# Four of five pairs kept raw at the border of two FFN stages, and the last pair's stores begun two steps later

## The chip, the cores and the metric

The kernel runs on one core of one Trainium2 chip. The metric is device time in microseconds: the median of three runs before the change is 2650.71 us (2648.62 to 2653.48). One execution was also recorded by the hardware profiler; durations, waits and transfers below are from it.

Engines: PE is TensorE (matmul; PEld its weight load), DVE is VectorE, ACT is ScalarE, POOL is GpSimd, and SP only issues transfers. Each engine works its instructions off in order, and so do the two queues of transfers, one issued by SP and one by POOL.

## The reference

One inference step of a one-layer encoder for 640 tokens (512 of a prompt and 8 x 16 samples), width 2048, in fp32:

```python
def merge_and_ffn(x, oa, ob, norm_grp_a, norm_grp_b, w_out, norm_ffn, w_gate, w_up, w_down):
    o = jnp.concatenate([rmsnorm(oa, norm_grp_a), rmsnorm(ob, norm_grp_b)], axis=-1)
    x = x + o @ w_out
    h = rmsnorm(x, norm_ffn)
    return x + (jax.nn.silu(h @ w_gate) * (h @ w_up)) @ w_down
```

Before this stands an input projection with two groups of attention heads, behind it a final norm. The change is in the last line: h @ w_gate and h @ w_up (FF1 here, 2048 to 5632) and the product with w_down (FF2, 5632 to 2048).

## The kernel before

**Split operands.** Every fp32 operand x is cut into two halves that are kept as float32r: hi = x rounded by an ACT copy, lo = x - hi by a subtraction on DVE. A product then takes three matmuls, hi x hi, hi x lo and lo x hi (`mm3`, lines 204, 205 and 206). Weights are split by `split` (line 195 on ACT, line 196 on DVE). Line 200 is the same subtraction with a gain, used elsewhere.

**Seven products for eight.** FF1 and FF2 multiply 2 x 2 blocks by a Strassen-Winograd scheme: `quartet` loads four weight blocks b11, b12, b21, b22 (line 907), forms their differences (lines 920 and 922 on DVE, 925 and 934 on POOL) and runs seven products p1, p6, p7, p2, p5, p4, p3. Each product splits its weight combination, runs k x 3 matmuls of 128x128 by 128x320 against operand number `which` (0 to 6), and yields. The caller then adds the product's bank into its results on DVE (line 944), copying the first one on ACT (line 1003 in FF1, 1084 in FF2).

**FF1.** The 44 row blocks of w_gate and w_up make 22 pairs i of two blocks. For each pair there is one quartet for w_gate and one for w_up, with k = 8: 168 matmuls each. After w_up, the gated result (lines 1030 to 1036) is turned into the seven Winograd combinations that FF2 needs as operands (lines 1040 to 1043 and in place); they are the seven `parts` of the pair, each 128x320 fp32, kept in S tiles.

**Storing parts.** `store_part` stores one part. It is called once when the parts have been formed, and from then on after the products of what follows (in FF1 all but p1, in FF2 all). For an ordinary pair it copies hi into a scratch tile of the tag "half" (line 985, ACT; the tag has two buffers), subtracts lo in place (line 987, DVE) and issues two transfers of 160 KB from SP into `act_d` (lines 988 and 989). For a pair in `raw_pairs` it issues one transfer of 160 KB into `first_d` (line 981) and splits nothing. The S tiles of a part go back to their list as soon as its store is emitted.

**FF2.** 32 steps. Step t works on 8 output rows q = t % 8 in turn, with the pairs in `active(t)`: five or six pairs, each staying for eight consecutive steps modulo 32. `active(0)` is [0, 1, 2, 3, 4]; pair 21, the last that FF1 forms, is first wanted in step 23, pair 0 again in step 25. With five pairs a product has k = 5, 15 matmuls, and a step 105. Operands stay in S tiles (hi and lo side by side) while their pair is active. When a pair comes in, `fetch` loads hi and lo together, 320 KB, by a transfer from POOL (line 951). In steps 0 to 7, x2 is loaded too (lines 1073 and 1074).

**The border.** While the last FF1 quartet runs, each of its seven products frees eight S tiles of h; `free(which)` (the hook `after` of that quartet) fills them with the operands `which` for step 0. Raw pairs are loaded from `first_d`, two to a transfer from SP (line 961, 320 KB; 160 KB where one is left over), and split by ACT (line 966) and, line 967, by DVE for the first of the two and POOL for the second. The others are fetched ready (line 951). Since a raw pair's halves were never stored, a raw pair that leaves in steps 0 to 7 is written to `act_d` then (line 1066, 320 KB from SP), as pairs 0 to 4 are wanted again in steps 25 to 31.

**What sets the order.** The source emits instructions, and the framework's planner orders them for each engine: an instruction with its operands ready may go ahead of one emitted before it on the same engine. It inserts the waits as well. Transfers from SP use eight completion counters in turn, so a transfer is issued only when the one eight before it has landed. Two rules bear on this place. `keep_turns` keeps the users of an S or W tile in their order. `keep_behind` ties each ACT copy of line 985 behind the ACT instruction emitted last before it, so that it can't go ahead of it.

Of the kernel before, what the change touches and what calls it, by code (L numbers as in the profile page):

```python
# [13 lines left out]
P = 128  # L14
# [3 lines left out]
HT = 320  # L18
# [15 lines left out]
def active(step):  # L34

    return [j for j in range(NPAIR) if (step - START[j]) % STEPS < 8]
# [13 lines left out]
class Net:  # L50
# [20 lines left out]
    def add(self, queue, work):  # L71
        self.queues.setdefault(queue, []).append(work)
# [209 lines left out]
def sh(t, *shape):  # L282
    v = t[:, :int(np.prod(shape))]
    if len(shape) == 2:
        v = v.rearrange("p (a b) -> p a b", a=shape[0])
    elif len(shape) == 3:
        v = v.rearrange("p (a b c) -> p a b c", a=shape[0], b=shape[1])
    return v
# [7 lines left out]
def r(ap):  # L296
    return ap.bitcast(F32R)


def build(nc, tc, io, pools):  # L300
# [14 lines left out]
    def dram(name, shape):  # L315
        return pools["dr"].tile(list(shape), F32, tag=name, name=name)
# [486 lines left out]
    own_b, acts_b = group_operands(ob_d, g_b, ssq, range(8))  # L803
    n.add("decode", decode_a(1))
    x2_d, act_d = dram("x2_d", (KT, P, TOK)), dram("act_d", (7, P, NPAIR, 2, HT))
    first_d = dram("first_d", (7, P, 3, HT))
    r_a, ssq_a = n.get("S"), n.get("S")
    for m in range(KT):
        ps = n.dense([(io["w_out_b"][m], 8)], acts_b)
# [141 lines left out]
        nc.gpsimd.dma_start(out=r(sh(t, 2, HT)), in_=r(act_d[which, :, j]))  # L951
        lefts[j][which] = t, hl

    raw_pairs = active(0)[1:4]

    def free(which):
        n.put("S", *(h[which][0] for h in hs))
# [18 lines left out]
    def store_part():  # L976

        if parts:
            j, which, src, done = parts.pop(0)
            if j in raw_pairs:  # L980
                dma(out=first_d[which, :, j - raw_pairs[0]], in_=src)
            else:
                at = n.emitted()
                hi = n.scratch()
                nc.scalar.activation(r(hi), src, AF.Identity)  # L985
                n.behind.append((at, n.emitted()))
                nc.vector.tensor_tensor(r(src), src, hi, ALU.subtract)  # L987
                dma(out=act_d[which, :, j, 0], in_=hi)
                dma(out=act_d[which, :, j, 1], in_=src)
            n.put("S", *done)  # L990

    gate = None
    for i in range(NPAIR):
        for src in ("w_gate", "w_up"):
# [5 lines left out]
            for step, bank in quartet(8, load, hs, (lambda w: next(prep)) if start else None, free if end else None,  # L1000
                                      eng=nc.vector if start else nc.gpsimd):
                if step == "p1":
                    nc.scalar.activation(c11, bank, AF.Identity)
                elif step == "p6":
                    y.append(n.get("S"))
                    c12, c22 = y[1][:, :HT], y[1][:, HT:]
                    add(c12, c11, bank)
                elif step == "p7":
                    add(c21, c12, bank)
                elif step == "p5":  # L1010
                    add(c22, c21, bank)
                    add(c12, c12, bank)
                elif step == "p2":
                    add(c11, c11, bank)
                elif step == "p4":
                    add(c21, c21, bank)
                elif step == "p3":
                    add(c12, c12, bank)
                if step != "p1":
                    store_part()  # L1020
# [31 lines left out]
    def fetch_waiting(left):  # L1052
        while len(waiting) > left:
            for j, which in waiting.pop(0):
                fetch(j, which)

    def step(t, part="all"):
        now = active(t)
        nxt = active(t + 1) if t + 1 < STEPS else []
        cnt, q, last = len(now), t % 8, t >= STEPS - 8  # L1060

        def after(which):
            gone = [j for j in now if j not in nxt]
            for j in gone:
                if j in raw_pairs and t < 8:
                    dma(out=act_d[which, :, j], in_=sh(lefts[j][which][0], 2, HT))
            n.put("S", *(lefts[j][which][0] for j in gone))
            waiting.append([(j, which) for j in nxt if j not in now])
            fetch_waiting(2)

        if t < 8:
            x, y = n.get("S"), n.get("S")
            dma(out=x, in_=x2_d[q])
            dma(out=y, in_=x2_d[q + 8])
            sums.append((x, y, n.get("S") if q % 2 == 0 else sums[-1][2]))
        x, y, u = sums[q]
        c11, c21, c12, c22 = x[:, :HT], x[:, HT:], y[:, :HT], y[:, HT:]
        us = u[:, HT * (q % 2):HT * (q % 2) + HT]
        o = 2 * sum(len(active(i)) for i in range(q, t, 8))
        load = lambda z: io["w_down"][q + 8 * (z % 2), :, o + cnt * (z // 2):o + cnt * (z // 2) + cnt]  # L1080
        for name, bank in quartet(cnt, load, [lefts[j] for j in now], None, after, part):
            if name == "p1":
                if t < 8:
                    nc.scalar.activation(us, bank, AF.Identity)
                else:
                    add(us, us, bank)
                add(c11, c11, bank)
            elif name == "p6":
                add(us, us, bank)
                if last:  # L1090
                    for c in (c21, c22, c12):
                        add(c, c, us)
            elif name == "p7":
                add(c21, c21, bank)
                add(c22, c22, bank)
            elif name == "p5":
                add(c22, c22, bank)
                add(c12, c12, bank)
            elif name == "p2":
                add(c11, c11, bank)  # L1100
            elif name == "p4":
                add(c21, c21, bank)
            elif name == "p3":
                add(c12, c12, bank)
            store_part()
            yield name

    def run(*args):
        for _ in step(*args):
            pass  # L1110
# [39 lines left out]
    for name in step(STEPS - 2, "late"):  # L1150
        if name == "p2":
            next(norm)
# [107 lines left out]
```

## Time and profile before

| | |
|---|---|
| median of 3 runs | 2650.71 us (2648.62 to 2653.48) |
| profiled execution | 2653.13 us, its span 2651.3 us |
| PE busy | 2586.9 us (98%), 17565 matmuls |
| DVE, ACT, POOL busy | 1982.9, 1069.5, 658.9 us |
| FF1's last quartet, border and step 0 | about 2022 to 2095 us |
| DMA bytes | 388.47 MB, mean 147 GB/s |

The span runs from the first to the last instruction that the profiler recorded. The profile has a page (busy times, 40 slices of the span, the chain of work that ended last, the costliest groups of instructions, transfers) and views of the trace: busy times of each engine in chosen stretches, waits summed by who waited for whom, groups of instructions by line, and instructions in order of time. In their rows "dn" and "at" are PSUM banks, S and W are the tiles of operands and of weights, "half" is the scratch tile, x_d is x2_d.

### The profile page before, as it was taken

The page shows a single profiled execution, that of the slowest core. Times are in us where ns is not written, and L with a number is a line of the kernel's source. Part 1 is how long each engine was busy: PE and PEld are TensorE (multiplying, and loading weights), DVE is VectorE, ACT ScalarE, POOL GpSimd, SP SyncE. Part 2 cuts the span into 40 slices and gives each one's busy share as a digit, 9 for nine tenths or more (in the row PEclk, how much of TensorE's full clock was granted, in tenths as well). Part 3 has the DMA queues.
Part 4 walks back from the last instruction along what each step waited for, and adds up shares of the span by engine and source line. Part 5 has one row for each costly group of instructions (what it writes and reads, how often), then busy time and mean ns, then how long its engine had stood idle before and what let it go on. Part 6 is the DMA issues. An engine that isn't in the chain of part 4 may idle for free.

```text
span 2651.3 us, 45161 instructions
## 1 busy us (share of the span) xinstructions
PE 2586.9 (98%) x17565; PEld 2529.9 (95%) x17565; DVE 1982.9 (75%) x3071; ACT 1069.5 (40%) x1732; POOL 658.9 (25%) x576
## 2 busy tenths in 40 slices
PE   8999999999999999999999999999999799999997
PEld 8999998999899999999999999999999799999996
DVE  5665566655866888778888888888887677777797
ACT  5443344444633544333343443433444333333343
POOL 0000000000211203333333333233234432333353
PEclk9999999999999999999999999999999899999998
DMA  5322232433655433333443433433436975665655
GB/s 172 105 71 80 89 104 85 131 115 132 219 184 187 157 120 122 116 104 124 139 133 123 142 130 125 141 131 124 148 126 215 365 206 151 176 185 163 189 154 179
DMA packets 178390, 388.47 MB, mean 147 GB/s; under 512 B 21696, under 2 KB 70208, under 8 KB 178176
## 3 DMA queue, kind: packets, MB, share of 16 engines
q1 hardware_dynamic: 152832, 329.22, 38.4%
q0 software_dynamic: 24192, 55.06, 7.4%
q8 instruction: 138, 2.26, 0.3%
q10 hardware_dynamic: 1152, 1.31, 0.1%
q14 instruction: 76, 0.62, 0.1%
HBM read 301.90 MB, written 82.87 MB: 145 GB/s over the span
## 4 chain that ended last, share of the span: by engine, by line
PE 70%; DVE 6%; DMA 5%; issue 2%; ACT 1%; POOL 0%; SPq 0%; DVEq 0%; ACTq 0%; POOLq 0%
PE dn L204 14%; PE dn L206 14%; PE dn L205 14%; PE at L204 8%; PE at L205 8%; PE at L206 8%; DVE W L196 2%; DMA W<-w_down 2%; PE at L319 1%; DVE S L944 1%; DMA act_d<-half 1%; ACT W L195 0%; DMA S<-first_d 0%; DMA S<-x_d 0%; PE at L395 0%
## 5 line engine op out<-in xcount | busy, mean ns | idle before, releaser
L204 PE MATMUL dn<-S,W 128*128 128x320 f32 x3694 | 1160.9, 314 | 6.2 <-ACT W L195 4.8
L206 PE MATMUL dn<-S,W 128*128 128x320 f32 x3694 | 1148.1, 311 | 17.7 <-DVE W L196 17.7
L205 PE MATMUL dn<-S,W 128*128 128x320 f32 x3694 | 1146.5, 310 | 1.4 <-DVE S L200 1.0
L195 ACT ACTIVATE W<-W 128x1024 fp32r<-128x1024 f32 (+2 forms) x632 | 608.1, 963 | 977.3 <-PE dn L205 533.6
L196 DVE TENSOR_TENSOR W<-W,W 128x1024 fp32r<-128x1024 f32 (+2 forms) x632 | 740.6, 1172 | 91.9 <-ACT W L195 88.2
L206 PEld LDWEIGHTS dn<-S,W 128*128 128x128 f32 x3694 | 695.7, 188 | 23.1 <-DVE W L196 22.0
L204 PEld LDWEIGHTS dn<-S,W 128*128 128x128 f32 x3694 | 696.3, 189 | 18.2 <-ACT W L195 5.8
L205 PEld LDWEIGHTS dn<-S,W 128*128 128x128 f32 x3694 | 696.1, 188 | 4.2 <-DVE S L200 1.6
L204 PE MATMUL at<-S,W 128*128 128x320 f32 x1594 | 494.6, 310 | 5.6 <-ACT W L195 5.6
L206 PE MATMUL at<-S,W 128*128 128x320 f32 x1594 | 495.3, 311 | 2.3 <-DVE W L196 2.2
L205 PE MATMUL at<-S,W 128*128 128x320 f32 x1594 | 494.1, 310 | 0.0
L925 POOL TENSOR_TENSOR W<-W,W 128x1024 f32<-128x1024 f32 (+2 forms) x75 | 158.9, 2119 | 650.2 <-DVE W L196 381.4
L204 PEld LDWEIGHTS at<-S,W 128*128 128x128 f32 x1594 | 300.1, 188 | 6.1 <-ACT W L195 6.1
L206 PEld LDWEIGHTS at<-S,W 128*128 128x128 f32 x1594 | 300.0, 188 | 4.7 <-DVE W L196 4.5
L205 PEld LDWEIGHTS at<-S,W 128*128 128x128 f32 x1594 | 300.1, 188 | 0.0
L944 DVE TENSOR_TENSOR S<-S,dn 128x320 f32<-128x320 f32 x358 | 163.9, 481 | 71.6 <-PE dn L206 71.6
L934 POOL TENSOR_TENSOR W<-W,W 128x1024 f32<-128x1024 f32 (+2 forms) x75 | 162.4, 2165 | 114.8 <-DVE W L196 108.6
L920 DVE TENSOR_TENSOR W<-W,W 128x1024 f32<-128x1024 f32 (+2 forms) x76 | 127.1, 1672 | 69.3 <-DMA W<-w_down 33.8
L944 DVE TENSOR_TENSOR S<-S,at 128x320 f32<-128x320 f32 x262 | 123.4, 481 | 50.7 <-PE at L206 50.0
L951 POOL DMA_DIRECT2D S<-act_d x168 | 91.7, 547 | 185.2 <-PE dn L206 92.7
L922 DVE TENSOR_TENSOR W<-W,W 128x1024 f32<-128x1024 f32 (+2 forms) x76 | 82.2, 1081 | 64.7 <-DMA W<-w_up 34.6
L987 DVE TENSOR_TENSOR S<-S,half 128x320 fp32r<-128x320 f32 x133 | 115.0, 886 | 14.7 <-ACT half L985 12.9
(152 smaller groups left out, 2129.2 us busy)
## 6 DMA issues: line engine op xcount, KB each, us to landing
S<-act_d POOLq DMA_DIRECT2D x168, 320.0 KB, 3.8
W<-w_gate SPq DMA_DIRECT2D x88, 512.0 KB
W<-w_up SPq DMA_DIRECT2D x88, 512.0 KB
W<-w_in SPq DMA_DIRECT2D x66, 512.0 KB
W<-w_down SPq DMA_DIRECT2D x64, 384.0 KB
W<-w_down SPq DMA_DIRECT2D x68, 320.0 KB
act_d<-half SPq DMA_DIRECT2D x133, 160.0 KB
act_d<-S SPq DMA_DIRECT2D x133, 160.0 KB
```

The source lines that it names most:

```text
L195: self.nc.scalar.activation(hi, src, AF.Identity)
L196: self.nc.vector.tensor_tensor(lo, src, f(hi), ALU.subtract)
L204: mm(out, a[0], b[0], start=first, stop=False)
L205: mm(out, a[0], b[1], start=False, stop=False)
L206: mm(out, a[1], b[0], start=False, stop=last)
L920: nc.vector.tensor_tensor(b12[:, w], b12[:, w], b22[:, w], sub)
L922: nc.vector.tensor_tensor(s6[:, w], b11[:, w], b12[:, w], sub)
L925: eng.tensor_tensor(b11[:, w], b22[:, w], s6[:, w], sub)
L934: eng.tensor_tensor(b21[:, w], b21[:, w], s6[:, w], sub)
L944: add = lambda o, a, b: nc.vector.tensor_tensor(o, a, b, ALU.add)
L951: nc.gpsimd.dma_start(out=r(sh(t, 2, HT)), in_=r(act_d[which, :, j]))
L987: nc.vector.tensor_tensor(r(src), src, hi, ALU.subtract)
```

## The change

```diff
@@ -803,7 +803,7 @@
-    first_d = dram("first_d", (7, P, 3, HT))
+    first_d = dram("first_d", (7, P, 4, HT))
@@ -951,7 +951,7 @@
-    raw_pairs = active(0)[1:4]
+    raw_pairs = active(0)[1:]
@@ -1102,7 +1102,8 @@
             elif name == "p3":
                 add(c12, c12, bank)
-            store_part()
+            if t > 1:
+                store_part()
             yield name
```

Two things change. Pair 4 joins pairs 1, 2 and 3 as a raw pair: in FF1 its seven parts are stored unsplit, one transfer each; at the border it comes as the second of a transfer (pairs 1 and 2, then pairs 3 and 4) and is split by ACT and POOL; and its halves are written to `act_d` when it leaves after step 6. Pair 0 alone is fetched ready for step 0. Second, of the last pair's seven parts the first is stored at the end of FF1, as it was; the other six, stored after products of step 0, are now stored after the products of step 2.

## The prediction

> **What bounds the kernel now.** I read the page first.
>
> ```profile
> span 2651.3 us, 45161 instructions
> PE 2586.9 (98%) x17565; PEld 2529.9 (95%) x17565; DVE 1982.9 (75%) x3071; ACT 1069.5 (40%) x1732; POOL 658.9 (25%) x576
> ...
> PE   8999999999999999999999999999999799999997
> ...
> PEclk9999999999999999999999999999999899999998
> GB/s 172 105 71 80 89 104 85 131 115 132 219 184 187 157 120 122 116 104 124 139 133 123 142 130 125 141 131 124 148 126 215 365 206 151 176 185 163 189 154 179
> ```
>
> TensorE (PE) is busy throughout except at the ends and in slice 32 (2055 to 2121 us), where the granted clock drops too and the DMA engines move 365 GB/s against some 130 before it. That is the border between FF1 and FF2, where the change works. Next the busy times by stretch. I cut them at the last FF1 quartet, the gap after it, step 0 (ended by the copy of step 1's first product at 2095.5) and the steps behind. Columns: stretch, length, then busy time and count of each engine, granted clock, DMA share, GB/s.
>
> ```profile
> 2022.00:2060.60 38.60, 33.45 (x209) 31.65 (x207) 27.04 (x33) 17.65 (x32) 26.44 (x28) 0.96 0.89 303
> 2060.60:2064.10 3.50, 0.06 (x1) 0.09 (x1) 3.43 (x6) 1.26 (x3) 2.83 (x4) 0.94 1.11 385
> 2064.10:2095.50 31.40, 21.47 (x110) 19.88 (x111) 18.49 (x29) 8.19 (x15) 13.51 (x20) 0.79 1.10 371
> 2095.50:2111.80 16.30, 15.68 (x107) 15.42 (x106) 11.90 (x19) 5.57 (x10) 3.69 (x3) 1.00 0.99 332
> 2111.80:2128.70 16.90, 15.85 (x106) 15.13 (x105) 11.76 (x18) 5.52 (x10) 5.77 (x7) 1.00 0.97 328
> 2128.70:2145.60 16.90, 16.90 (x117) 16.90 (x117) 12.36 (x21) 5.89 (x10) 5.50 (x7) 1.00 0.75 214
> ```
>
> In the last row PE never stops: 16.90 / 117 = 0.1444 us for a matmul. At that rate the other stretches lose: quartet 38.60 - 209 x 0.1444 = 8.4 us; gap 3.4; step 0 31.40 - 110 x 0.1444 = 15.5; step 1 0.8; step 2 1.6. Together 29.7 us, and half of it lies in step 0. Who waits for whom from 2060 to 2095.5, and on the DMA queue's side, says why (us in total, times, longest):
>
> ```profile
> ACT half L985 <- DMA act_d<-half: 17.0, 4, 7.4
> DVE S L987 <- ACT half L985: 12.9, 5, 6.7
> ...
> PE at L204 <- ACT W L195: 5.1, 1, 5.1
> ...
> PE dn L206 <- DVE W L196: 4.3, 3, 3.3
> ...
> PE dn L204 <- ACT W L195: 3.5, 1, 3.5
> ...
> ACT half L985 <- DVE S L1036: 2.4, 1, 2.4
> ...
> PE at L206 <- DVE W L196: 0.5, 1, 0.5
> ```
>
> ```profile
> SPq L988 <- ACT half L985: 15.5, 5, 5.2
> ```
>
> The parts of the last pair are stored here. L985 copies one into a scratch tile; there are two scratch tiles, so it waits until an earlier store out of that tile has landed. ACT, DVE and the SP queue work in order, and behind L985 stand the weight splits (L195, L196) that PE waits for, behind L988 the loads of w_down. The chain in order of time shows the turns:
>
> ```profile
> 2062.84 0.48 ACT half L985
> ...
> 2063.75 9.20 DMA S<-x_d
> ...
> 2073.02 10.74 DMA act_d<-half
> ...
> 2083.85 0.48 ACT half L985
> ...
> 2084.34 5.45 DMA act_d<-half
> ...
> 2090.79 0.82 DVE W L922
> ```
>
> So a transfer takes 5 to 11 us while the DMA engines are full, and each holds up three queues.
>
> **The parts in step 0, removed.** Six of the seven parts leave it: 6 copies on ACT, 6 subtractions on DVE, 12 SP transfers of 160 KB, moved behind the w_down and x2 loads of steps 0 to 2. The first part (2062.84) stays at the end of FF1, and with it the 3.5 us gap. PE's waits from 2060 sum to 5.1 + 4.3 + 3.5 + 0.5 = 13.4; without the 3.5 that stays, 9.9 lie in step 0. Its loss is 15.5, so 5.6 us are the lower clock (0.79). I leave the gap's share of that, 3.5 / 13.4 x 5.6 = 1.5. The rest goes: **-14.0 us**. Bounds: -15.5 and 0 (if the loads, and not the parts, turn out to set the pace).
>
> What is late next are the w_down loads. In steps 1 and 2, without any part, at 332 and 328 GB/s, PE lost 0.8 and 1.6 us, and DVE's waits from 2095 to 2130 name the cause:
>
> ```profile
> DVE W L920 <- DMA W<-w_down: 6.7, 2, 3.6
> ```
>
> With the transfers of steps 0 to 2 pushed together I take nearly as much once more, **+2.0** (0 to +11.9, which is 14.0 less the 2.1 that the first rival leaves).
>
> **The parts in step 2, added.** The same 6 + 6 + 12 instructions, one behind each product from step 2 on; an ACT copy can't be pulled ahead, since it is tied behind the ACT work written before it. Behind it on ACT stand the splits of step 2. In FF1, 1200 to 2000 us, the same wait occurs without harm:
>
> ```profile
> ACT half L985 <- DMA act_d<-half: 48.6, 19, 3.7
> ```
>
> ```profile
> L204 PE MATMUL dn<-S,W 128*128 128x320 f32 x1039 | 321.6, 310 | 0.0
> ```
>
> Waits up to 3.7 us cost PE 0.0 there, as splits run ahead of it; the 7.4 us of step 0 did cost. Below: 0, since added work wins nothing. Above: all 14.0 return. Step 2 at 328 GB/s lies between, nearer the free case since w_down waits there are at most 3.6: **+1.5**. The three S tiles that the parts hold through two steps only delay fetches made far ahead: 0.
>
> **The border, pair 4 split instead of fetched.** Rows by line, 2020 to 2135, and ACT's wait:
>
> ```profile
> L951 POOL DMA_DIRECT2D S<-act_d x41 | 22.5, 556 | 21.6 <-DVE W L920 10.7 <-PE at L206 5.4 <-PE dn L206 2.9
> ...
> L967 DVE TENSOR_TENSOR S<-S,S 128x320 fp32r<-128x320 f32 x14 | 10.5, 758 | 10.8 <-ACT S L966 10.8
> ...
> L966 ACT ACTIVATE S<-S 128x320 fp32r<-128x320 f32 x21 | 9.1, 464 | 21.1 <-DMA S<-first_d 13.6 <-DMA act_d<-S 6.2 <-DVE S L967 1.2
> ...
> L967 POOL TENSOR_TENSOR S<-S,S 128x320 fp32r<-128x320 f32 x7 | 8.1, 1152 | 6.7 <-ACT S L966 6.7
> ```
>
> Added: 7 copies on ACT (7 x 0.464 = 3.2 us), 7 subtractions on POOL (7 x 1.152 = 8.1), and 7 raw loads grow from 160 to 320 KB. Removed: 7 fetches, 7 x 0.556 = 3.9 us of POOL and 2.29 MB. ACT has room (17.65 of 38.60), but it stands in order at L966 until a raw load lands, 13.6 us in all, and weight splits queue behind. What the SP queue moved there, 2026 to 2060:
>
> ```profile
> q1 hardware_dynamic: 3174, 6.09, 51.0%
> ...
> act_d<-S SPq DMA_DIRECT2D x6, 320.0 KB
> S<-first_d SPq DMA_DIRECT2D x6, 320.0 KB
> ...
> S<-first_d SPq DMA_DIRECT2D x7, 160.0 KB
> ```
>
> SP's share is 6.09 MB / 34 us = 0.179 MB/us, so 7 x 160 KB = 1.15 MB more could push the last raw tile back 6.4 us: the upper end. Below, all queues together carry 2.29 - 1.15 = 1.14 MB less, at 0.385 MB/us 3 us to the good. I take the quartet's loss in proportion to its splits, 8.4 x 7 / 21 = **+2.8**.
>
> **Elsewhere.** FF1 loses 7 copies, 7 subtractions and 7 of 14 stores for pair 4: 0, because PE idles 0.0 there (row above); nothing is due there. In FF2 pair 4 must be written once as two halves, 7 transfers of 320 KB on SP. By the text that is step 6, but the present 21 (pairs 1 to 3) go out far ahead of steps 2 to 5, where they stand; the first row below is of the whole run (durations, then first and last start), the second of 2060 to 2095. So some of the new seven will join the crowd: **+0.5**, and up to 2.29 / 0.179 = 12.8 if all go ahead of needed loads.
>
> ```profile
> L1066 SPq DMA_DIRECT2D act_d<-S x21: 319/430/969, 2026.9 to 2115.3; - x21
> ```
>
> ```profile
> act_d<-S SPq DMA_DIRECT2D x3, 320.0 KB
> ```
>
> **Sum.** -14.0 + 2.0 + 1.5 + 2.8 + 0.5 = -7.2 us. The profiled execution took 2653.13 (span 2651.3), which gives 2645.9; it is 2.4 above the median 2650.71, so for the median 2643.5.
>
> **Rivals.** First: *bytes, not the queues, set the pace.* For it: 385 and 371 GB/s around step 0, so unblocked queues merely meet a full DMA. Against: of the 41 fetches from 2020 to 2135 step 0 needs 14 (pairs 0 and 4), so much of that traffic isn't due. The border then gains what it no longer carries: 1.14 MB and the parts' 1.97 MB, less pair 4's 2.29 MB, 0.82 MB / 0.385 = 2.1 us: 2648.6.
>
> Second: *POOL's subtractions hold up DVE.* In the rows L967 averages 758 ns on DVE against 493 where it runs free, and 1152 on POOL against 884. Seven more of at least 0.88 us, each in front of an L196, would add 6.2: -1.0, 2649.7. Against: DVE has 11.6 us idle in the quartet. The Trainium skill, "SBUF — State Buffer", section "Who interferes with whom", speaks for this rival: a DVE instruction with two SBUF inputs and a GpSimd instruction that reads SBUF exclude each other, and the later one blocks in full. The stretched means here agree with it; by the rule alone the sum would be this rival's.
>
> ```profile
> L967 DVE TENSOR_TENSOR S<-S,S x14: 478/493/1861, 2026.4 to 2059.9; 128x320 fp32r<-128x320 f32 x14
> ...
> L967 POOL TENSOR_TENSOR S<-S,S x7: 872/884/1554, 2030.7 to 2057.5; 128x320 fp32r<-128x320 f32 x7
> ```
>
> Third, the other side: *pair 4's bytes fill the SP queue ahead of w_down.* All 1.15 + 2.29 = 3.44 MB come before the loads of steps 0 and 1: 3.44 / 0.179 = 19.2 us later, against 14.0 won, and 1.5 in step 2: +6.7, 2657.4. It decides from 14.0 x 0.179 = 2.5 MB ahead of those loads. For it: 6 of the present 21 stores were already issued by 2060. Against: 12 of the 21 came after 2095 (21 - 6 - 3), and fetches on POOL shrink by 2.29 MB, which leaves SP a larger share.
>
> Fourth: *nothing comes back*, neither in step 2 nor at the border: -14.0, 2636.7.
>
> That the parts are not moved at all is excluded by the tie on ACT.
>
> **Chances.** Forecast 0.50 (own range 2639 to 2648), bytes 0.18, POOL on DVE 0.07, SP queue 0.13, nothing back 0.12. What a measurement here tells from no change is 0.2%, 5.3 us, so faster means below 2645.4. Of the forecast some 0.44 lies below, with 0.12 of the fourth 0.56; same is 0.06 + 0.18 + 0.07 = 0.31; slower 0.13. The range 2635 to 2654 leaves out the third rival and little else.
>
> **What would show it.** Right: no L985 between 2064 and 2095; step 0 near 17 us instead of 31.4 with clock 0.95 or more; the quartet 2 to 4 us longer; L985 in step 2 with waits under 4 us and PE losing under 3 there. The L1066 issues say which rival holds: with most of 28 before step 1's w_down loads, the third; if step 0 still takes 25 us with PE behind DVE behind w_down, the first; POOL's L967 beside long L196, the second. I am wrong if step 0 stays long without parts, or if step 2 loses what step 0 gains.

## The result, and the profile after

The change makes the kernel slightly slower: 2656.72 us (median of 20 runs, 2649.64 to 2661.94) against 2652.31 (20 runs, 2648.21 to 2655.15) on the same chip. The ratio is 1.0017, with a 95% interval of 1.0011 to 1.0023: +4.4 us, where -7.2 had been forecast.

The profiled execution took 2654.09 us. Its page:

```profile
span 2652.3 us, 45136 instructions
...
PE 2589.7 (98%) x17565; PEld 2535.3 (96%) x17565; DVE 1978.8 (75%) x3064; ACT 1068.3 (40%) x1732; POOL 664.1 (25%) x576
...
PE   8999999999999999999999999999999899999997
...
GB/s 173 104 74 78 90 101 88 132 120 127 220 183 184 156 119 123 116 104 108 141 131 123 145 132 122 153 120 129 150 115 218 340 243 155 170 184 161 196 155 174
```

Slice 32, a 7 before, is an 8 now, and its transfers fell only from 365 to 340 GB/s.

The stretches, cut at the same times as in the prediction (length, busy time and count of PE, PEld, DVE, ACT and POOL, granted clock, DMA share, GB/s):

```profile
2022.00:2060.60 38.60, 31.13 (x189) 30.11 (x187) 37.27 (x35) 21.04 (x41) 29.63 (x28) 0.91 0.82 275
2060.60:2064.10 3.50, 2.63 (x10) 2.66 (x11) 3.43 (x6) 1.05 (x3) 3.49 (x7) 0.51 0.82 206
2064.10:2095.50 31.40, 24.69 (x144) 23.90 (x142) 16.59 (x25) 7.71 (x11) 11.90 (x16) 0.88 1.11 391
2095.50:2111.80 16.30, 15.47 (x89) 15.47 (x90) 12.06 (x21) 4.74 (x8) 3.71 (x3) 0.81 0.92 300
```

Two things stand out. The third row got 34 matmuls more than before (144 against 110), where the forecast's 14.0 us would be 97 more at 0.1444 us each, and its DMA engines still move 391 GB/s. And in the quartet DVE, 27.04 us busy before, is now busy for 37.27 of 38.60 us. (At this place after's execution runs 2.9 us ahead of before's, so equal times cut off slightly later work. Over the quartet's own matmuls DVE was busy 26.94 of 38.50 us before, and is busy 34.97 of 39.10 us now.) The waits from 2060 to 2095.5 have a new owner:

```profile
ACT W L195 <- DMA W<-w_down: 6.5, 1, 6.5
DVE W L920 <- DMA act_d<-S: 6.4, 1, 6.4
...
DVE W L922 <- DMA W<-w_down: 3.6, 1, 3.6
...
PE dn L204 <- ACT W L195: 3.2, 1, 3.2
...
PE dn L206 <- DVE W L196: 3.1, 1, 3.1
```

No wait of L985 for a transfer is left there. In its place ACT and DVE wait for w_down. The row that names a store (`act_d<-S`) misleads. L920 reads two loads of w_down; it waits on their two counters, and a write-out used one of these counters next. Its wait ended when the other of the two loads, issued at 2084.72, landed at 2094.62. The chain of waits in order of time ends step 0 the same way, with the same wrong name in its fifth line:

```profile
2068.19 9.82 DMA W<-w_down
2078.11 0.75 ACT W L195
2078.86 0.81 DVE W L196
2079.69 6.65 DMA W<-w_down
2086.36 8.38 DMA act_d<-S
2094.74 0.80 DVE W L920
2095.54 0.75 DVE W L196
2096.33 0.64 PE dn L206
```

**A finer yardstick.** All kernels here run the same 17565 matmuls, but for a handful in the same order, so for each one its start time can be set against that of the same matmul before. The table does so from matmul 13630 on (2022 us before), where the difference is put to zero; it is worked out from the matmuls' times in the traces, one execution of each kernel, so a us or two between rows proves nothing by itself. Negative is earlier; the columns stand at matmuls that before started at the time on top. The last column is the measured ratio less 1, times 2651 us.

```
                                quartet        step 0  step 1  step 2  step 3
                                 2060.1 2070.0 2095.5  2112.1  2130.0  2146.1  2220.1 | by the ratio
after (the change)                  0.6    1.7   -6.4    -0.8    -0.9     2.3     2.3 |   4.5
e1 pair 4 raw only                  2.0   -2.6   -4.4    -1.6    -3.3     0.9     0.9 |   0.0
e2 late parts only                  3.1    2.0   -4.9     1.6     0.0     6.3     6.3 |   6.9
e3 after, write-outs held           1.8    1.5  -10.8   -11.1   -12.8    -6.8    -4.6 |  -3.4
e4 before, write-outs held          0.1    0.2   -2.2    -2.1    -3.4    -2.1    -2.1 |  -1.1
e5 after, write-outs from POOL     -0.2    1.8   -9.3    -7.1    -4.0     0.3     0.3 |   1.6
e6 e3, parts in step 4              0.7    2.7  -10.5   -10.6   -11.8   -10.2    -3.4 |  -1.1
e7 e6, first part late too          3.2    0.2   -9.9   -10.8   -12.6   -11.7    -1.7 |  -3.7
e8 e6, three raw                   -0.7   -0.6  -10.1   -10.9   -11.5   -10.2    -6.0 |  -6.4
e9 e6, all subtractions on DVE      0.7   -3.3  -16.1   -16.6   -17.2   -15.7    -8.5 |  -9.0
e10 e8, first part late too        -0.6   -0.4  -11.6   -12.4   -14.2   -10.0    -4.9 |  -6.1
e11 e8, all subtractions on DVE     3.9   -0.2   -9.0    -9.9   -10.8    -9.3    -5.7 |  -6.1
e13 e2, write-outs held             1.3    1.7  -11.4    -8.3   -10.0    -3.0    -3.0 |  -4.5
e14 after, all subtractions on DVE  4.1   -0.2  -10.1    -9.2    -7.3    -3.4    -3.4 |  -1.6
e15 e9, first part late too         0.8   -3.2  -11.1   -12.0   -13.8   -11.9    -4.5 |  -6.6
```

The last two columns agree within 2.3 us in every row, so nearly the whole effect arises between 2022 and 2220 us. (The spans of the two profiled executions differ by 1.0 us only, because the profiled execution of before also lost some 3 us between 900 and 1000 us that after's did not lose; that stretch has nothing to do with the change.) The row "after" reads: step 0 gains 7.0 us (0.6 to -6.4), step 1 gives back 5.6 and step 3 another 3.2.

### The profile page after: what moved, and what is told of

The parts are those of the page before. It is cut to its first block, busy times and chain, and to the rows that moved or that the text cites. A ratio compares the mean times of both kernels' runs of the same rounds, so it can differ in the third digit from the quotient of the medians.

```text
span 2652.3 us, 45136 instructions
## 1 busy us (share of the span) xinstructions
PE 2589.7 (98%) x17565; PEld 2535.3 (96%) x17565; DVE 1978.8 (75%) x3064; ACT 1068.3 (40%) x1732; POOL 664.1 (25%) x576
## 4 chain that ended last, share of the span: by engine, by line
PE 70%; DVE 6%; DMA 5%; issue 1%; ACT 1%; POOL 1%; SPq 0%; DVEq 0%; ACTq 0%; POOLq 0%
PE dn L206 14%; PE dn L204 14%; PE dn L205 14%; PE at L204 8%; PE at L205 8%; PE at L206 8%; DMA W<-w_down 2%; DVE W L196 2%; PE at L319 1%; DVE S L944 1%; DMA act_d<-S 1%; DMA act_d<-half 1%; ACT W L195 1%; PE at L395 0%; DMA W<-w_gate 0%
## 5 line engine op out<-in xcount | busy, mean ns | idle before, releaser
L934 POOL TENSOR_TENSOR W<-W,W 128x1024 f32<-128x1024 f32 (+2 forms) x75 | 162.7, 2169 | 109.8 <-DVE W L196 102.5
L920 DVE TENSOR_TENSOR W<-W,W 128x1024 f32<-128x1024 f32 (+2 forms) x76 | 127.1, 1673 | 80.7 <-DMA W<-w_down 37.3
L987 DVE TENSOR_TENSOR S<-S,half 128x320 fp32r<-128x320 f32 x126 | 108.9, 886 | 4.1 <-ACT half L985 2.4
```

What stands on the lines that cost most here:

```text
L920: nc.vector.tensor_tensor(b12[:, w], b12[:, w], b22[:, w], sub)
L934: eng.tensor_tensor(b21[:, w], b21[:, w], s6[:, w], sub)
```

## The experiments

The theories: *the forecast's* (the parts' turns cost 14 us in step 0, pair 4 raw costs a little); *queue*: the write-outs of line 1066 stand in front of w_down on the SP queue and take the place of the parts; *bytes*: the DMA is full whatever the order; *POOL and DVE*: the added subtractions on POOL hold up DVE.

### One part of the change at a time

e1 keeps the fourth raw pair and puts the parts back into step 0; e2 keeps the late parts and has three raw pairs.

```diff
 e1 (against after)
-            if t > 1:
-                store_part()
+            store_part()
 e2 (against after)
-    first_d = dram("first_d", (7, P, 4, HT))
+    first_d = dram("first_d", (7, P, 3, HT))
-    raw_pairs = active(0)[1:]
+    raw_pairs = active(0)[1:4]
```

> The changed kernel with one half of the change alone: pair 4 raw, the last pair's parts stored from step 0 on as before. Theory A (the SP queue: in the border the loads of w_down stand behind write-outs of raw pairs, line 1066, and wait for the full DMA): seven write-outs more and 1.15 MB more raw loads, with the parts' turns of step 0 still there, so slower than the kernel before by 3 to 10 us, 2655 to 2662. Theory B (splitting pair 4 costs ACT, POOL and DVE time, the queue does not matter): 8.1 us of subtractions on POOL, +3 to +6, the loss lying in the last FF1 quartet and not in steps 0 to 3. The prediction's terms: +2.8 + 0.5 = +3.3.

> The kernel before with the other half alone: pairs 1 to 3 raw, parts stored from step 2 on. The prediction's terms: -14.0 + 2.0 + 1.5 = -10.5 us, about 2642. Theory A: the places of the parts on the SP queue are taken by write-outs and the wait for w_down takes the place of the parts' wait, so -4 to +3, 2648 to 2655, with no L985 between 2064 and 2095 and PE waiting for L196 behind w_down instead. Theory B: about -10, as in the prediction, since pair 4 is fetched ready here.

Measured: e1 2652.61 us, ratio 1.0000 (0.9991 to 1.0009). e2 2657.40 us, 1.0026 (1.0015 to 1.0036). Both theories for e1 had expected a loss, and e2 is slower than both of its ranges. So the loss comes with the late parts, the half of the change that was to bring all of the gain. Where it comes from is told by the issues of line 1066 between 2064 and 2091 us (durations, then first and last start), in before, after and e2 in turn:

```profile
L1066 SPq DMA_DIRECT2D act_d<-S x2: 320/371/422, 2064.7 to 2068.4; - x2
```

```profile
L1066 SPq DMA_DIRECT2D act_d<-S x10: 320/438/669, 2064.1 to 2086.4; - x10
```

```profile
L1066 SPq DMA_DIRECT2D act_d<-S x9: 319/430/512, 2063.7 to 2085.0; - x9
```

While the parts took their turns on SP, they held back the write-outs as well as the loads. With the parts gone, eight more write-outs of 320 KB, not due before steps 27 to 31, go out among the loads of step 0. The SP queue of after in order of time (start, duration, line, transfer) shows how they stand:

```profile
2079.69 0.33 SPq L907 DMA_DIRECT2D W<-w_down  x1
2080.06 0.43 SPq L1074 DMA_DIRECT2D S<-x_d  x1
2080.54 1.85 SPq L1066 DMA_DIRECT2D act_d<-S  x4
2084.72 0.33 SPq L907 DMA_DIRECT2D W<-w_down  x1
2085.10 1.58 SPq L1066 DMA_DIRECT2D act_d<-S  x2
2088.79 0.33 SPq L907 DMA_DIRECT2D W<-w_down  x1
```

One load, four write-outs, one load, two write-outs, one load: 4 to 5 us from load to load. The planner put them there, since their operands are ready. The write-outs do not keep the loads from being issued, though: SP has issued the four by 2082.4 and then stands until 2084.72. What most issues of w_down wait for is a split of earlier weights that frees their W tile (the SP queue's own waits, 2060 to 2140):

```profile
SPq L907 <- DVE W L196: 25.0, 9, 4.7
```

What the write-outs lengthen is the time from a load's issue to its landing. It can be read from the counters in each trace for the same six loads of steps 1 and 2, issued between 2060 and 2092: in after they took 6.7 to 9.9 us, 8.6 on average, and in e2 9.3 on average.

### The write-outs held back

To test this, each transfer of line 1066 is tied behind the SP instruction emitted last before it (other than a write-out), so that it can't go ahead of a load emitted earlier. Its lines are marked, and a function modelled on `keep_behind` adds the dependencies:

```diff
 e3 (against after), e4 (against before)
+                    at = n.emitted()
                     dma(out=act_d[which, :, j], in_=sh(lefts[j][which][0], 2, HT))
+                    n.late.append((at, n.emitted()))
...
+    n.keep_late()
...
+    def keep_late(self):
+        info = mybir.DependencyInfo(mybir.DependencyClass.NoSync, mybir.DependencyReason.DATA)
+        for k, block in enumerate(self.nc.cur_f.blocks):
+            inside = [0] * (len(block.instructions) + 1)
+            for a, b in self.late:
+                if k < len(a):
+                    inside[a[k]:b[k]] = [1] * (b[k] - a[k])
+            last = None
+            for i, ins in enumerate(block.instructions):
+                if ins.engine == mybir.EngineType.SP:
+                    if not inside[i]:
+                        last = ins
+                    elif last is not None:
+                        self.tc.add_manual_dep(ins, last.name, info, reason="late")
```

Sixteen lines are added, so that in these kernels line 195 is 211, 204 is 220, 206 is 222, 907 is 923, 920 is 936, 944 is 960, 967 is 983, 985 is 1001, 1036 is 1052 and 1066 is 1083.

> The changed kernel with its 28 write-outs of raw pairs (line 1066) tied behind the SP transfer emitted last before them, so that they go out in steps 2 to 6 and not in the border; nothing else is changed. Theory A: the w_down loads of steps 0 to 2 land in time, the losses there fall from some 20 us to under 8, and the kernel takes 2640 to 2648, below both. Theory B: the write-outs are not the cause, 2654 to 2658 as the changed kernel.

> The kernel before with its 21 write-outs of raw pairs tied in the same way. The parts are still stored in step 0. Theory A: less stands in the DMA rings in step 0, so the parts land sooner and their turns hold up ACT less: 2643 to 2650. If the write-outs take no time from anything, 2652. If the order as such is to blame and not the bytes, e3 and e4 gain the same.

Measured: e3 2647.77 us, ratio 0.9987 (0.9978 to 0.9996), 8 us better than after. e4 2650.56 us, 0.9996 (0.9988 to 1.0005): in before the hold brings nothing that can be told from no change. In e3's trace two write-outs are left in that stretch, and step 0 has 194 matmuls, with 303 GB/s instead of 391. The six loads land 5.3 us after their issue on average, where after had 8.6:

```profile
L1083 SPq DMA_DIRECT2D act_d<-S x2: 425/456/488, 2084.2 to 2090.1; - x2
```

```profile
2064.10:2095.50 31.40, 30.17 (x194) 29.14 (x194) 24.80 (x38) 9.94 (x14) 13.33 (x16) 0.97 0.91 303
2095.50:2111.80 16.30, 16.30 (x113) 16.30 (x113) 14.98 (x26) 7.58 (x14) 2.95 (x4) 1.00 0.78 246
2111.80:2128.70 16.90, 12.41 (x76) 12.15 (x75) 6.61 (x13) 3.39 (x5) 7.17 (x10) 0.90 1.08 393
```

The last row shows the bill: in step 3 of e3 (a few us earlier than before's) parts and held write-outs come together: SP issues 12 transfers of parts and 12 write-outs between 2098 and 2118, and two loads of w_down among them. The DMA is full again at 393 GB/s, ACT waits 5.0 us for a w_down load, and PE has a gap of 4.65 us behind it. e13 is e2 with the same lines added:

```diff
 e13 (against e2)
+                    at = n.emitted()
                     dma(out=act_d[which, :, j], in_=sh(lefts[j][which][0], 2, HT))
+                    n.late.append((at, n.emitted()))
...
+    n.keep_late()
```

> e2 (three raw pairs, parts from step 2) with the write-outs held, nothing else. Theory A: what e2 lost by write-outs ahead of w_down comes back and the parts' 14 us are won, 9 to 13 us faster than e2, 2644 to 2648; against e3 it has pair 4 fetched ready, by which it should be 2 to 5 us faster than e3. If parts in step 2 cost by themselves, 2650 or more.

Measured: 2647.34 us, ratio 0.9983 (0.9974 to 0.9991), against e2's 1.0026: 11 us; its six loads took 6.2 us on average, where e2's took 9.3. With two pairs of kernels, one mechanism is shown: parts out of step 0 pay only if the write-outs stay out of it too. With three raw pairs all four cases are measured, and they also say how much: without the hold the late parts cost 7 us (e2 against before), with it they win 3 (e13 against e4, 0.9983 and 0.9996, intervals overlapping).

Is it the place in the SP queue, or the bytes? e5 leaves the write-outs as early as they are, but issues them from POOL.

```diff
 e5 (against after)
-                    dma(out=act_d[which, :, j], in_=sh(lefts[j][which][0], 2, HT))
+                    nc.gpsimd.dma_start(out=act_d[which, :, j], in_=sh(lefts[j][which][0], 2, HT))
```

> The changed kernel with its 28 write-outs of raw pairs issued by POOL instead of SP. The same 9.2 MB are moved, as early as before, but no longer in the SP queue ahead of w_down. If the place in the SP queue is what delays the w_down loads (theory A1), 2643 to 2650. If the full DMA engines delay them wherever the bytes come from (theory A2), 2654 to 2660, and PE waits for L196 behind w_down as in the changed kernel.

Measured: 2651.76 us, ratio 1.0006 (0.9997 to 1.0015). That is 3 us below after, with intervals that overlap, and 5 above e3. The table shows step 0 nearly as short as e3's (-9.3) and then 9.6 us given back in steps 1 to 3. Its time lies between the two theories, and so do its six loads, with 7.1 us on average between after's 8.6 and e3's 5.3. So it seems that the place in the SP queue is part of it and the bytes under way, whichever queue issues them, another; how much of the rest is POOL, which has 28 more issues to do, these runs don't separate.

### The parts later still

e6 moves the six parts from step 2 to step 4, in which no pair of `raw_pairs` leaves, in order to keep them clear of the write-outs. e7 delays the first part with them, and so takes its copy out of the gap at the end of FF1.

```diff
 e6 (against e3)
-            if t > 1:
+            if t > 3:
                 store_part()
 e7 (against e6), behind the last part of FF1
-                store_part()
+                if not end:
+                    store_part()
```

> e3 (write-outs held) with the six parts stored from step 4 on instead of step 2; step 4 has no write-outs of its own. If the 4.65 us gap that e3 has left at 2121 us comes from parts and write-outs meeting in steps 2 and 3, it goes: 3 to 6 us faster than e3, 2641 to 2645. If the write-outs alone make it, as e3, 2646 to 2649.

> e6 with the first part, stored at the end of FF1 until now, also put off to step 4. If its copy (line 985) makes PE's gap of 3.1 to 3.6 us between FF1 and step 0, with the slow clock behind it, 3 to 5 us faster than e6, 2637 to 2641. If PE would wait there for the last weight splits anyway, within 1.5 us of e6.

Measured: e6 2648.47 us, 0.9996 (0.9987 to 1.0004): not better than e3, so the expected gain is missed. But e6 doesn't test whether the meeting with the write-outs was what cost, since they meet again: tied behind loads that go out early, the write-outs go out ahead of the steps in which they are written. The seven of pair 3, written in step 5, were issued between 2136 and 2147, and the parts' twelve transfers between 2132 and 2143. e7 2646.36 us, 0.9986 (0.9976 to 0.9995), 2.7 us below e6 with intervals that overlap, between its two theories. The table says why e6 didn't gain: the big gap of step 3 is gone, but 7 us come back behind 2146, in steps 5 and 6. Between 2130 and 2220 the kernels with held write-outs and late parts give back 8.2 (e3), 8.4 (e6), 7.0 (e13) and 5.5 us (e8): later stores don't become free stores. In e9, treated below, this stretch has the DMA full at 395 GB/s and PE at 76 matmuls where 104 fit:

```profile
2155.00:2170.00 15.00, 12.01 (x76) 11.00 (x75) 7.89 (x13) 5.40 (x8) 5.84 (x7) 1.00 1.07 395
```

### What pair 4 costs, and the two engines that split it

e8 is e6 with three raw pairs; e10 is e8 with the first part late too, by e7's edit.

```diff
 e8 (against e6)
-    first_d = dram("first_d", (7, P, 4, HT))
+    first_d = dram("first_d", (7, P, 3, HT))
-    raw_pairs = active(0)[1:]
+    raw_pairs = active(0)[1:4]
 e10 (against e8)
-                store_part()
+                if not end:
+                    store_part()
```

> e6 with three raw pairs as before the change (pairs 0 and 4 fetched ready). The prediction's terms for pair 4, +2.8 and +0.5, say that this is 3 us faster than e6. If bytes in the border count most, it is 2 to 4 us slower, since 1.14 MB more are fetched for step 0. If pair 4 makes no difference, as e6.

> e8 (three raw pairs, write-outs held, parts from step 4) with the first part put off as well. If its copy makes the 3.6 us gap between FF1 and step 0, 2 to 4 us faster than e8, 2640 to 2642. If PE waits there for the last weight splits anyway, as e8, 2643 to 2644.

Measured: e8 2643.60 us, ratio 0.9976 (0.9967 to 0.9985); e10 2645.16 us, 0.9977 (0.9968 to 0.9986). The first part's place makes no difference here. The fourth raw pair costs 5 us (e6 against e8, 0.9996 and 0.9976); with the parts in step 2 it was 1 us, within the error (e3 against e13). What about it costs? In e6 DVE's rows of 2022 to 2060 (columns: busy us, mean ns, idle before) have the border's subtractions at 1248 ns on average and one weight difference at 3856 ns; POOL has 14 subtractions beside them:

```profile
L983 DVE TENSOR_TENSOR S<-S,S 128x320 fp32r<-128x320 f32 x14 | 17.0, 1248 | 3.9 <-ACT S L982 3.9
...
L936 DVE TENSOR_TENSOR W<-W,W 128x640 f32<-128x640 f32 x1 | 3.9, 3856 | 0.0
```

```profile
L983 POOL TENSOR_TENSOR S<-S,S 128x320 fp32r<-128x320 f32 x14 | 15.9, 1146 | 0.1
```

So e9 takes them off POOL and gives all 28 to DVE, the busier engine; e11 does it with three raw pairs, e14 to the change as it is, e15 to e9 with the first part late.

```diff
 e9 (against e6), e11 (against e8), e14 (against after)
-                (nc.vector, nc.gpsimd)[a].tensor_tensor(lo, part, f(hi), ALU.subtract)
+                nc.vector.tensor_tensor(lo, part, f(hi), ALU.subtract)
 e15 (against e9)
-                store_part()
+                if not end:
+                    store_part()
```

> e6 (four raw pairs, write-outs held, parts from step 4) with all 28 subtractions of the border on DVE, where e6 gives the second of each two to POOL. If DVE and POOL hold each other up there (theory C; in e6 the DVE subtractions of line 967 average 1248 ns, and one L920 took 3.9 us), DVE's busy time in the last quartet falls from 37 to about 30 us although it has 14 more instructions, and the kernel is 2 to 5 us faster than e6, 2643 to 2647. If DVE's own work is the limit, 28 x 0.48 = 13.4 us there make it slower by 1 to 4, 2649 to 2652.

> e8 with all 21 subtractions of the border on DVE. Theory C: seven POOL instructions fewer that hold up DVE, 1 to 3 us faster than e8, 2640 to 2643. If DVE's own work is the limit, 1 to 2 us slower.

> The changed kernel with one edit: all 28 subtractions of the border on DVE; write-outs not held, parts from step 2. Theory C with A: the last quartet is mended as in e9 (8 us against e6 there), the write-outs still stand ahead of w_down, so 4 to 8 us faster than the changed kernel, 2648 to 2652, no more than level with the kernel before. If the write-outs hide the gain (what the quartet wins is lost again to w_down in steps 0 to 3), as the changed kernel, 2654 to 2658.

> e9 with the first part put off to step 4 too. e10 showed no gain from that with three raw pairs, e7 some 2 us with four. If the first part's copy holds up the splits behind it, 1 to 3 us faster than e9, 2640 to 2642; if not, as e9, 2643.

| | us | ratio (95%) | same with POOL |
|---|---|---|---|
| e9, four raw, held | 2643.25 | 0.9966 (0.9954 to 0.9979) | e6 0.9996 (0.9987 to 1.0004) |
| e14, the change, not held | 2647.88 | 0.9994 (0.9985 to 1.0002) | after 1.0017 (1.0011 to 1.0023) |
| e11, three raw, held | 2644.95 | 0.9977 (0.9967 to 0.9986) | e8 0.9976 (0.9967 to 0.9985) |
| e15, e9 with the first part late | 2643.07 | 0.9975 (0.9965 to 0.9984) | e7 0.9986 (0.9976 to 0.9995) |

With four raw pairs the one word is worth 8 us (e9), 6 us (e14) and perhaps 3 (e15, intervals overlapping); with three raw pairs, nothing, where 1 to 3 us had been expected. DVE's rows of e9 in the same stretch:

```profile
L983 DVE TENSOR_TENSOR S<-S,S 128x320 fp32r<-128x320 f32 x28 | 14.7, 575 | 4.7 <-ACT S L982 4.7
...
L936 DVE TENSOR_TENSOR W<-W,W 128x640 f32<-128x640 f32 x1 | 0.8, 819 | 0.0
```

Twice the subtractions take less time than half of them beside POOL: 14.7 us for 28 against 17.0 for 14. DVE's timeline shows where that decides. First e6, then e9:

```profile
2054.24 5.94 DVE L983 TENSOR_TENSOR S<-S,S 128x320 fp32r<-128x320 f32 x3
2060.11 0.47 DVE L960 TENSOR_TENSOR S<-S,at 128x320 f32<-128x320 f32 x1
2060.61 0.82 DVE L1052 TENSOR_TENSOR S<-S,S 128x640 f32<-128x640 f32 x1
```

```profile
2052.01 2.10 DVE L983 TENSOR_TENSOR S<-S,S 128x320 fp32r<-128x320 f32 x5 [0.53 <-ACT S L982]
2054.03 0.48 DVE L960 TENSOR_TENSOR S<-S,at 128x320 f32<-128x320 f32 x1
```

In e6 three subtractions take 5.94 us just ahead of the end of FF1, beside three of POOL's and one weight difference there, and PE then stands for 4.6 us before FF2's first product. The waits of 2056 to 2064 in e6 name the way from the one to the other:

```profile
PE dn L220 <- ACT W L211: 4.4, 1, 4.4
ACT half L1001 <- DVE S L1052: 4.4, 1, 4.4
```

L1052, a step in forming the parts, comes on DVE behind the three subtractions; ACT's copy of the first part (L1001) waits for it, and the weight split (L211) that PE needs stands on ACT behind the copy. In e6 this L1052 begins 2.4 us after the quartet's last matmul, in e9 (at 2054.83) 6.6 us before it. e9 goes over from FF1 to FF2 without a gap; its last gap in the quartet, 3.3 us, ended 3.6 us before. By the start of step 0 it is 4.3 us ahead of e6 (-2.7 against 1.6), at 2070 6.0. Its step 0 loses next to nothing:

```profile
2064.10:2095.50 31.40, 30.60 (x207) 29.94 (x206) 24.00 (x37) 10.80 (x16) 11.17 (x13) 1.00 0.95 324
```

e9 is faster than before and after, by 9 us against before (five runs). e14's 6 us came another way: its quartet is 3.5 us longer than after's, with a gap of 7.8 us, and at the start of step 0 it is level with after (0.7 against 0.3). It wins 4.2 us in step 0 and 4.6 in step 1 and gives 2.7 back later; which waits these are stays open. Nor do these runs tell DVE's relief from POOL's, whose own queue became shorter too (30.32 us busy over the quartet in e6, 20.89 in e9). Whether the fourth raw pair helps once it is on DVE stays open (e9 0.9966 and e11 0.9977, intervals overlapping), and so does the first part: e15 isn't told apart from e9.

## Why the prediction was wrong

**The parts in step 0, -14.0: right, on a condition that was missed.** From 2060 to 2095.5 the yardstick gives -12.6 with the write-outs held (e3), and -16.8 with the subtractions off POOL as well (e9). The hold alone, with the parts still there, gives -2.3 (e4), so the parts' own share is about 10 us in e3 and e13. The change itself got -7.0. The parts' turns were a real cost, as read from the waits of L985 and L988; but they were also a brake on transfers that nobody needed yet.

**What is late next, +2.0: the step that failed.** "What is late next are the w_down loads" was right; its size was not. Against e3's -12.6, the change is short of 5.6 us in step 0 and loses 5.6 more in step 1, where PE waits for the chain shown above: about 11, near the upper bound of 11.9. (e3 pays some of it back later, so that the hold is worth 8 us in all.) What the runs showed in place of 2.0 are loads that land 8.6 us after their issue, where e3 has 5.3. The value was read from steps 1 and 2 of before. There 12 write-outs went out too, but with six fetches from POOL beside them, at some 330 GB/s; with the parts gone, 11 write-outs met 11 fetches in step 0, at 391 GB/s. The estimate took the next obstacle's size from a stretch in which the first obstacle still kept the two apart.

**Pair 4's write-out, +0.5.** "Some of the new seven will join the crowd" saw the crowd, and the issue row showed 12 of the 21 after 2095; that the old 21 would come forward once SP was free was left out of the sum without a reason. This is close to the third rival's mechanism, write-outs ahead of w_down, but with other bytes: it needs no fourth raw pair (e2 has three and is at 1.0026), so the rival's 3.44 MB of pair 4 were not what decided. It named the right side and, with 2657.4, came closest to the time, which was partly luck.

**The parts in step 2, +1.5.** The waits of the copy were as small as said:

```profile
ACT half L985 <- DMA act_d<-half: 5.4, 4, 1.9
```

and step 2 lost nothing against before. But step 3 lost 3.2 us in after: there DVE waits 4.6 us for a load that was issued behind the parts' twelve transfers and a late write-out and took 6.8 us to land. The parts' share of that isn't separated from the write-outs'. Counted with the write-outs, 5 to 11 us come back between 2130 and 2220 in all kernels that have both the hold and the gain of step 0, so this term was too small also where the rest held, and the three terms of the late parts, -10.5 together, came to -3 even with the hold (e13 against e4).

**Pair 4 at the border, +2.8.** By the end of the quartet 0.6 us, with the gap behind it 1.7: within the bounds. What the fourth raw pair costs in all depends on what stands beside it: from nothing (e1, e3 against e13; after is even 2 us below e2) to 5 us (e6 against e8), and only the last is clear of the noise. So +2.8 is neither confirmed nor refuted. Where it did cost, with the parts in step 4, the second rival's mechanism is in the traces: with the subtractions off POOL, e9 is 8 us faster than e6, 5 by the yardstick; that is for all 14 that POOL had, where the rival had +6.2 for the seven added. The prediction gave it 0.07, against it "DVE has 11.6 us idle in the quartet". Idle time was no cover: in after DVE is busy 34.97 of 39.10 us over the quartet's matmuls. Its subtractions of 2022 to 2060, at 758 ns before, take 1113; POOL's are twice as many at much the same 1173 (DVE's row, then POOL's):

```profile
L967 DVE TENSOR_TENSOR S<-S,S 128x320 fp32r<-128x320 f32 x14 | 15.2, 1113 | 3.9 <-ACT S L966 3.8
```

```profile
L967 POOL TENSOR_TENSOR S<-S,S 128x320 fp32r<-128x320 f32 x14 | 16.2, 1173 | 0.1
```

And one L920, 0.82 us where it runs alone, took 3.59 (DVE's timeline, then POOL's):

```profile
2034.65 3.59 DVE L920 TENSOR_TENSOR W<-W,W 128x640 f32<-128x640 f32 x1 [0.21 <-DMA W<-w_down]
```

```profile
2032.91 2.27 POOL L967 TENSOR_TENSOR S<-S,S 128x320 fp32r<-128x320 f32 x2
2035.14 2.40 POOL L934 TENSOR_TENSOR W<-W,W 128x1024 f32<-128x1024 f32 x1
```

It lies beside POOL's L967 and L934 and ends within a us of the latter. The Trainium skill, "SBUF — State Buffer", section "Who interferes with whom", says that a DVE instruction with two SBUF inputs and a GpSimd instruction that reads SBUF exclude each other, the later one blocking in full; the trace agrees, with 3.59 us against 0.82 for the same instruction elsewhere. That pair 4 raw alone is at 1.0000 (e1) fits neither +2.8 nor this price by itself: with the parts still in step 0, e1 gains there (-2.6 already at 2070, -4.4 at 2095.5) and gives it back in steps 1 and 3; its copies wait 9.5 us in all in step 0, three times, against 17.0 in four before. Why e1 gains there stays open.

**The first rival, bytes.** Its sign of 391 GB/s in a step 0 that stays long is in the trace, and e3 reaches 194 matmuls at 303 GB/s by leaving out what isn't due, which changes order and bytes at once. e5 keeps the bytes and changes the queue, and gets some 3 of e3's 8 us, with 393 GB/s from 2064 to 2095.5. So the rival was partly right: bytes ahead of their time cost the loads as well as their place in the queue, and in what shares stays open. Bytes also count where they are paid later (the 395 GB/s row). **The fourth**, nothing back, falls: in no kernel did a gain of 7 us or more in step 0 stay whole.

**FF1 and the S tiles, 0** each: the yardstick places all but 2.3 us of every result within 2022 to 2220, so the first stands; and no wait of PE from 2015 to 2230 names a fetch in any of these kernels, so nothing speaks against the second.

## What to carry to other kernels

When a stall is removed, ask what it was holding back as well as what it delayed: whatever the planner may pull forward will be pulled into the freed queue, so transfers that aren't due have to be tied behind those that are, in the same edit. Read the size of the next obstacle from a stretch that the first one does not shape. And where DVE and GpSimd share short SBUF-to-SBUF work at the bottleneck, expect a subtraction on GpSimd to stretch those on DVE; giving all of it to the busier engine may free both.

## What the runs showed of the hardware

With 14 subtractions of 128x320 taken from POOL and given to DVE, DVE did 51 instructions in the quartet in the time of 30: 34.32 us busy (e9), where it had been 35.27 (e6). The rows of the quartet's own matmuls, which in e6 begin 3.1 us earlier than in e9, e6 and then e9:

```profile
2019.20:2058.20 39.00, 32.57 (x207) 31.59 (x206) 35.27 (x30) 20.06 (x39) 30.32 (x28) 0.96 0.76 249
```

```profile
2022.30:2061.40 39.10, 32.80 (x208) 31.75 (x207) 34.32 (x51) 21.20 (x41) 20.89 (x24) 0.94 0.90 313
```

Stretching went as far as 3.86 us (e6) for an instruction of 0.82, and 5.94 us for three that take 0.42 each in e9 (2.10 / 5).

A transfer that is issued by another queue is not out of the way: with the write-outs on POOL, step 0 came within 1.5 us of e3's at 2095.5, and 9.6 us were lost behind it; from 2080 to 2100 the DMA moved 401 GB/s:

```profile
2080.00:2100.00 20.00, 16.96 (x112) 16.21 (x112) 13.87 (x23) 6.22 (x9) 10.71 (x17) 1.00 1.08 401
```

A gap of PE costs more than its length. Behind the 3.39 us gap in e9 that ends at 2171.3 some 15 matmuls started up to 0.27 us apart instead of 0.147, 1.6 us more, and in the stretch that holds it the granted clock is 0.89:

```profile
2170.00:2185.00 15.00, 13.68 (x83) 13.68 (x84) 10.94 (x18) 4.02 (x6) 4.76 (x5) 0.89 0.53 149
```
